# A hybrid trunk on one core: norms' exponential ahead of the decays', spans behind the scaling, and a rearranged last batch of the delta rule

## The chip, the cores and the metric

The kernel runs on one core of one Trainium2 chip. The metric is device microseconds (us) of that core for one launch. Work is done by TensorE (PE; matmuls and, overlapped, weight loads, PEld), VectorE (DVE), ScalarE (ACT), GpSimd (POOL) and by DMA queues, of which SyncE's (SP) carries the weights. Each engine takes its own instructions strictly in order and waits for others through semaphores.

## The reference

A chunk-causal encoder with two layers, sequence 256, width 2048, float32: differential attention, a gated MLP with a causal convolution (ConvFFN), a gated DeltaNet layer, another ConvFFN. The change is in the DeltaNet layer:

```python
proj = h @ w_in                                    # q, k, v, z, and two small gates
qkv = silu(causal_dwconv(qkv, conv_w))
q, k = l2_norm(q), l2_norm(k)                      # 16 heads of 128, each shared by 2 value heads
beta, g = sigmoid(b_gate), -exp(a_log) * softplus(a_gate + dt_bias)
# gated_delta_rule, per value head, in chunks:
g_c = cumsum(g)
decay = exp(where(tril, g_c[:, None] - g_c[None, :], -inf))
low = where(strict, (k * beta) @ k.T * decay, 0)
u, w = triangular_solve(low + eye, v * beta), triangular_solve(low + eye, k * beta * exp(g_c))
...                                                # o: a scan over chunks with a running state
o = rms_norm(o, norm_g) * silu(z)
return o @ w_out
```

## The kernel before

All large products run in three passes (high part of the weight times low and high part of the activation, low part of the weight times high part). Weights stream from HBM in chunks of 512 KB: a load `raw` on SP's queue (L100), a CAST on ACT to `whi` (L111), a subtraction on DVE to `wlo` (L112), then 24 matmuls on PE at L150, L151 and L152 (`ps<-h`, or `ps<-oc` in the DeltaNet's output projection). Four buffers of each rotate. After each chunk `tick` (L81) lets the small tasks that were spawned as generators go on by one step, up to their next `yield`; after a `yield RUN` a task goes on only on every second tick, in the last batch's end on every tick (`self.period`). The steps so put into the program are then ordered per engine by the framework's scheduler. So PE works through weight matmuls with short stretches of small products in between, and the distance from one stretch of a task to its next is a count of weight matmuls.

In `gdn` (L565) the 16 query/key heads are done in four batches (`nb`) of four (`hb`), and in each batch come: four projections for q and k, each followed by a spawned `keys`; a projection for v; two for the gate z; three more for v. After a batch, the output projection `out` of the batch before runs; after the last batch also its own. The tasks:

- `keys(hq, ...)` squares q and k of a head (`cv`, tile `qs`), splits the squares (L323, L324), sums them on PE (L331), takes logarithms (L638, L639) and the exponential (L640) on ACT, and scales `cv` by the result (L645, DVE). PE's products L652 and L653 need the scaled `cv`. Beside this the decays: `gb` is loaded from DRAM on SP's queue (L623, one buffer), DVE makes the spans `d` from it (L633), and ACT takes their exponentials (L643, L644). The products are multiplied by `d` into `lt` and `qkt` (L658, L659).
- `invert` and `join` solve the triangular systems of all heads of a batch, on DVE and then on PE (L718, L727, L741, L750).
- `to_tokens` turns v to tokens (PE L763, ACT L764) and appends to the list `ready`. 
- `group` (two heads, four value heads; two groups in a batch) makes the outputs: products L781, copies L786 and L793, squares L804, sums L805, reciprocal root by Ln and Exp (`rsqrt`, L318, L319), the gate by `zt` (L815), transposes L826, and the split of the result into `oc` (L831 on ACT, L832 on DVE), which the output projection multiplies.

`lnexp` (L297) loads the activation table that holds both Ln and Exp (shown at L299) behind a named instruction and puts what stands in its block behind that load; table loads that other functions need are put in where the order wants them and appear under the line of the function.

Of the kernel before, what the change touches and what calls it, by code (L numbers as in the profile page):

```python
# [8 lines left out]
F32 = mybir.dt.float32  # L9
F32R = mybir.dt.float32r  # L10
AF = mybir.ActivationFunctionType
ALU = mybir.AluOpType
# [4 lines left out]
P = 128  # L17
T = 256
# [11 lines left out]
class Trunk:  # L30
# [38 lines left out]
    def mp(self):  # L69
        return self.mps.tile([P, 512], F32, tag="mp", name="mp")  # L70
# [494 lines left out]
    def gdn(self, w_gate, w_in, w_z, w_out, nb, hb, gate_ap, const_ap, fold_ap, conv_col, ng, done):  # L565
# [7 lines left out]
        nc, tc, mp = self.nc, self.tc, self.mp  # L573
# [4 lines left out]
        with tc.tile_pool(name="gd", bufs=1) as gd:  # L578
# [4 lines left out]
            ident, mask, triu = con[:, :P], con[:, P:T], con[:, T:]  # L583
# [30 lines left out]
            def keys(hq, c, cc, b0, res):  # L614

                sq = gd.tile([P, 2, T], F32, tag="qs", name="qs", bufs=2)
                nc.scalar.square(sq, c)
                sp = gd.tile([P, 2, 2, T], F32R, tag="qp", name="qp", bufs=1)
                self.split(sp, sq)
                while "col" not in gates:  # L620
                    yield
                gb, gc = gd.tile([P, 2 * T], F32, tag="gb", name="gb", bufs=1), gates["col"]
                nc.sync.dma_start(gb.rearrange("p (v t) -> p v t", v=2),  # L623
                                  decays[2 * hq:2 * hq + 2, :].unsqueeze(0).to_broadcast([P, 2, T]))
                yield
                yield
                ds = []
                for v in range(2):
                    h = 2 * hq + v
                    g = gb[:, v * T:(v + 1) * T]  # L630
                    d = gd.tile([P, 384], F32, tag="d", name="d", bufs=2)
                    for t in range(2):
                        nc.vector.scalar_tensor_tensor(  # L633
                            d[:, (1 - t) * P:(2 - t) * P], g[:, t * P:(t + 1) * P], gc[:, t, h:h + 1], mask, ALU.add, ALU.add)
                    ds.append(d)
                pn = mp()
                with self.lnexp(self.total(pn, [sp])):
                    nc.scalar.activation(sq[:, 0, :], pn[:, :T], AF.Ln, bias=eps128, scale=float(P))  # L638
                    nc.scalar.activation(sq[:, 1, :], pn[:, T:], AF.Ln, bias=self.eps, scale=1.0)  # L639
                    nc.scalar.activation(sq, sq, AF.Exp, scale=-0.5)  # L640
                    for v, d in enumerate(ds):
                        h = 2 * hq + v
                        nc.scalar.activation(d[:, :T], d[:, :T], AF.Exp)  # L643
                        nc.scalar.activation(d[:, T:], gb[:, v * T + P:(v + 1) * T], AF.Exp, bias=gc[:, 0, h:h + 1])  # L644
                nc.vector.tensor_tensor(c, c, sq, ALU.mult)  # L645
                q, k = c[:, 0, :], c[:, 1, :]
                yield
                yield RUN
                prods = []
                for r in (k, q):  # L650
                    p = mp()
                    self.nc.tensor.matmul(p[:, :P], k[:, P:], r[:, P:], start=True, stop=True)  # L652
                    self.nc.tensor.matmul(p[:, P:384], k[:, :P], r, start=True, stop=True)  # L653
                    prods.append(p)
                for v in range(2):
                    lt = gd.tile([P, 384], F32, tag="lt", name="lt", bufs=2 * hb)
                    qkt = gd.tile([P, 384], F32, tag="qkt", name="qkt", bufs=2 * hb)
                    nc.vector.tensor_tensor(lt, prods[0][:, :384], ds[v], ALU.mult)  # L658
                    nc.vector.tensor_tensor(qkt, prods[1][:, :384], ds[v], ALU.mult)  # L659
                    b = b0 + v  # L660
                    lv = lt[:, :T].rearrange("p (t c) -> p t c", t=2)
                    for r in quad:
                        nc.gpsimd.tensor_copy(
                            cc[r, :, 2 * b:2 * b + 2].rearrange("p c t -> p t c"), lv[r, :, r])
                    res.append((lt, qkt))

            def invert(cc, lqs, mark):

                while len(lqs) < 2 * hb:
                    yield  # L670
                x = gd.tile([P, 32, 32], F32, tag="s4", name="X", bufs=3)
                nc.vector.transpose(x.rearrange(flat), cc.rearrange(flat))
                t = gd.tile([P, 32, 32], F32, tag="s4", name="Ti", bufs=3)
                nc.vector.tensor_scalar(t, x, -1.0, None, ALU.mult)
                nc.vector.memset(t.rearrange(flat)[:, ::33], 1.0)
                for j in range(1, 31):
                    m = 31 - j
                    tmp = gd.tile([P, T], F32, tag="tmp", name="tmp", bufs=1)
                    w = tmp[:, :m * j].rearrange("p (i c) -> p i c", c=j)
                    nc.vector.tensor_tensor(  # L680
                        w, x[:, j + 1:, j:j + 1].to_broadcast([P, m, j]),
                        t[:, j:j + 1, :j].to_broadcast([P, m, j]), ALU.mult)
                    nc.vector.tensor_tensor(t[:, j + 1:, :j], t[:, j + 1:, :j], w, ALU.subtract)
                    if j % 3 == 0:
                        yield
                ttc = gd.tile([P, 32, 32], F32, tag="s4", name="ttc", bufs=3)
                nc.vector.transpose(ttc.rearrange("p m i -> p i m"), t)
                tcc = gd.tile([P, 32, 32], F32, tag="s4", name="tcc", bufs=3)
                nc.vector.transpose(tcc.rearrange("p m c -> p c m"), t.rearrange("p i c -> p c i"))
                yield from join(lqs, ttc, tcc, mark)  # L690

            using, joined = set(), []

            def join(lqs, ttc, tcc, mark):

                while using:
                    yield
                nm = 2 * gv
                sets = range(len(lqs) // gv)
# [67 lines left out]
            def group(gi, gr, lqs, mark, vt, ready, zts, acts):  # L767

                TT = TTs[gi]
                n = 2 * len(gr)  # L770
# [22 lines left out]
                nc.scalar.copy(w1[:, :n, :], prod([(lambda v: TT[:, 2 * v, :], r1)]))  # L793
                using.discard((mark, gi))
                s = gd.tile([P, 2, gv], F32, tag="os", name="os", bufs=2)
                os = []
                for t in range(2):
# [6 lines left out]
                    nc.scalar.square(sq[:, :n, :], o)  # L804
                    last = nc.vector.tensor_reduce(s[:, t, :n], sq[:, :n, :], AX.X, ALU.add)  # L805
                    os.append(o)
                with self.lnexp(last):
                    self.rsqrt(s[:, :, :n], s[:, :, :n], P)
                while gi not in zts:
                    yield  # L810
                ys = []
                for t in range(2):
                    y = zts[gi][:, t]
                    for v in range(n):
                        nc.vector.scalar_tensor_tensor(  # L815
                            y[:, v, :], os[t][:, v, :], s[:, t, v:v + 1], y[:, v, :], ALU.mult, ALU.mult)
                    ys.append(y)
                yield
                yield RUN
                turned = {}  # L820
# [25 lines left out]
            for b in range(nb):  # L846
                heads = range(b * hb, (b + 1) * hb)
                cc = gd.tile([P, 32, 32], F32, tag="s4", name="Cc", bufs=3)
                nc.gpsimd.memset(cc, 0.0)
                lqs, acts, zts, ready = [], [], {}, []  # L850
                groups = [range(i, i + gh) for i in range(0, hb, gh)]
                plan = [("k", i) for i in range(hb)] + [("v", 0)] + [("z", g) for g in range(len(groups))]
                for op, i in plan + [("v", i) for i in range(1, hb)]:
                    last = b == nb - 1 and op != "k"
                    self.period = 1 if last else 2
                    if op == "k":
                        hq = heads[i]
                        c = convs(lin(self.dense(w_in[hq * 2], KD, self.h_acts, HP)), (hq, nq + hq))
                        self.spawn(keys(hq, c, cc, 2 * i, lqs))
                        if i == hb - 1:  # L860
                            self.spawn(invert(cc, lqs, b))
# [232 lines left out]
```

## Time and profile before

| | us |
|---|---|
| median of 3 runs | 2635.73 (2634.09 to 2637.54) |
| the profiled execution's own time | 2632.3 |
| its span | 2630.5 |
| PE busy | 2619.4 |
| DVE busy | 1835.5 |
| ACT busy | 1444.2 |

In the rows of the timelines, the columns are the start in us, the duration, engine, line and operation, the tile written and the tiles read, shapes, and the count of instructions that the row puts together; a bracket gives the time the engine was idle ahead of it and what released it. In the rows of waits: engine, tile and line that waited, what it waited for, us in total, times, the longest.

### The profile page before, as it was taken

Reading aid. Unit: us, or ns where it says so; the run is one execution under the profiler, and the core shown is the slowest. Engines: PE = TensorE matmul, PEld = TensorE weight load, DVE = VectorE, ACT = ScalarE, POOL = GpSimd, SP = SyncE. Lnnn points to the kernel's source line nnn. Section 1 sums busy time; section 2 is a strip of 40 time slices with the busy share of each in tenths; the row PEclk is TensorE's granted clock in tenths of the full one; section 3 lists DMA queues with packets and bytes.
Section 4 is the critical chain, followed back from the end, with each engine's and each line's share of the span. In section 5 each row is a group of like instructions: output and inputs, shape, how many; then the busy total and the mean of one; then the engine's idle time right before and its main releaser. Section 6 shows DMA issues by size and latency. Waiting matters only on the chain.

```text
span 2630.5 us, 53532 instructions
## 1 busy us (share of the span) xinstructions
PE 2619.4 (100%) x22302; PEld 2561.7 (97%) x22302; DVE 1835.5 (70%) x2718; ACT 1444.2 (55%) x1990; POOL 93.2 (4%) x188
## 2 busy tenths in 40 slices
PE   9999999999999999999999999999999999999999
PEld 9998899999999999999989989989999999999999
DVE  7866667777777555679688787688677777776444
ACT  6665555555555444485764664664555555554333
POOL 0000000000000000011011011021000000000000
PEclk9999999999999999999999999999999999999999
DMA  7565566666666666656455465565466666666665
GB/s 247 168 176 169 163 198 194 194 193 194 193 196 195 190 196 194 188 173 199 137 183 178 137 192 162 164 184 169 143 192 195 195 194 193 193 194 200 199 203 152
DMA packets 138100, 485.34 MB, mean 185 GB/s; under 512 B 15712, under 2 KB 19584, under 8 KB 137856
## 3 DMA queue, kind: packets, MB, share of 16 engines
q1 hardware_dynamic: 137280, 481.42, 60.2%
q8 instruction: 174, 2.85, 0.4%
q14 instruction: 70, 0.57, 0.1%
q10 hardware_dynamic: 576, 0.49, 0.1%
HBM read 479.72 MB, written 2.13 MB: 183 GB/s over the span
## 4 chain that ended last, share of the span: by engine, by line
PE 98%; ACT 1%; DVE 1%; DMA 1%; issue 0%; SPq 0%; DVEq 0%; ACTq 0%
PE ps L150 27%; PE ps L151 27%; PE ps L152 27%; PE ps L237 10%; PE mp L781 1%; PE ps L194 1%; PE mp L331 1%; PE mp L653 0%; PE mp L741 0%; PE mp L750 0%; PE mp L763 0%; PE mp L652 0%; PE mp L471 0%; PE mp L509 0%; DMA raw<-w_first 0%
## 5 line engine op out<-in xcount | busy, mean ns | idle before, releaser
L112 DVE TENSOR_TENSOR wlo<-raw,whi 128x1024 fp32r<-128x1024 f32 (+1 forms) x903 | 1100.6, 1220 | 607.2 <-ACT whi L111 604.3
L111 ACT CAST whi<-raw 128x1024 fp32r<-128x1024 f32 (+1 forms) x903 | 943.9, 1047 | 998.9 <-PE ps L151 829.4
L151 PE MATMUL ps<-h,whi 128*128 128x256 f32 x4224 | 1167.7, 276 | 0.0
L150 PE MATMUL ps<-h,whi 128*128 128x256 f32 x4224 | 1167.7, 276 | 0.0
L152 PE MATMUL ps<-h,wlo 128*128 128x256 f32 x4224 | 1167.4, 276 | 0.0
L152 PEld LDWEIGHTS ps<-h,wlo 128*128 128x128 f32 x4224 | 792.9, 188 | 1.1
L151 PEld LDWEIGHTS ps<-h,whi 128*128 128x128 f32 x4224 | 792.9, 188 | 1.0
L150 PEld LDWEIGHTS ps<-h,whi 128*128 128x128 f32 x4224 | 792.9, 188 | 1.0
L152 PE MATMUL ps<-ac,wlo 128*128 128x256 f32 x1632 | 450.4, 276 | 0.0
L151 PE MATMUL ps<-ac,whi 128*128 128x256 f32 x1632 | 450.4, 276 | 0.0
L150 PE MATMUL ps<-ac,whi 128*128 128x256 f32 x1632 | 450.2, 276 | 0.0
L151 PEld LDWEIGHTS ps<-ac,whi 128*128 128x128 f32 x1632 | 306.4, 188 | 0.0
L152 PEld LDWEIGHTS ps<-ac,wlo 128*128 128x128 f32 x1632 | 306.4, 188 | 0.0
L150 PEld LDWEIGHTS ps<-ac,whi 128*128 128x128 f32 x1632 | 306.2, 188 | 0.0
L237 PE MATMUL ps<-whi,h 128*128 128x512 f32 x768 | 240.1, 390 | 0.0
L237 PEld LDWEIGHTS ps<-whi,h 128*128 128x128 f32 x768 | 143.7, 188 | 30.2
L237 PE MATMUL ps<-wlo,h 128*128 128x512 f32 x384 | 149.8, 390 | 0.0
L150 PE MATMUL ps<-oc,whi 128*128 128x256 f32 x512 | 143.5, 280 | 1.6 <-DVE oc L832 1.6
L151 PE MATMUL ps<-oc,whi 128*128 128x256 f32 x512 | 143.1, 279 | 0.0
L312 DVE SCALAR_TENSOR_TENSOR cv<-u,fcols,cv 128x255 f32<-128x255 f32 (+1 forms) x344 | 142.8, 477 | 0.0
L152 PE MATMUL ps<-oc,wlo 128*128 128x256 f32 x512 | 142.2, 278 | 0.0
L157 DVE TENSOR_TENSOR u<-ps,rstd 128x512 f32<-128x512 f32 x118 | 81.5, 690 | 47.5 <-PE ps L152 47.2
(213 smaller groups left out, 2043.9 us busy)
## 6 DMA issues: line engine op xcount, KB each, us to landing
raw<-w_up SPq DMA_DIRECT2D x344, 512.0 KB, 4.4
raw<-w_down SPq DMA_DIRECT2D x160, 512.0 KB, 3.7
raw<-w_in SPq DMA_DIRECT2D x128, 512.0 KB, 4.2
raw<-w_z SPq DMA_DIRECT2D x64, 512.0 KB, 3.9
raw<-w_out SPq DMA_DIRECT2D x64, 512.0 KB, 3.7
raw<-w_qk SPq DMA_DIRECT2D x56, 512.0 KB, 4.2
raw<-w_v SPq DMA_DIRECT2D x32, 512.0 KB, 3.6
raw<-w_o SPq DMA_DIRECT2D x32, 512.0 KB, 4.3
```

The lines of the kernel that those rows point to most:

```text
L111: self.cast = nc.scalar.copy(hi, raw)
L112: self.low = nc.vector.tensor_tensor(lo, raw, hi.bitcast(F32), ALU.subtract)
L150: nc.tensor.matmul(o, hi[:, k, s], a[:, 1, :], start=first, stop=False)
L151: nc.tensor.matmul(o, hi[:, k, s], a[:, 0, :], start=False, stop=False)
L152: nc.tensor.matmul(o, lo[:, k, s], a[:, 0, :], start=False, stop=last)
L157: self.nc.vector.tensor_tensor(u, ps[:, :, :T], self.rstd.unsqueeze(1).to_broadcast([P, 2, T]), ALU.mult)
L194: self.nc.tensor.matmul(pss[c // 2][:, c % 2, :T], l[:, k, c * P:(c + 1) * P], acts(k0 + k)[:, i, :], start=k0 + k == 0 and l is hi and i ...
L237: self.nc.tensor.matmul(ps[:, c, :], l, r[:, k, :], start=first and not j, stop=last and j == 2)
L312: nc.vector.scalar_tensor_tensor(out[:, j:], u[:, :T - j], taps[n - 1 - j], out[:, j:], ALU.mult, ALU.add)
L331: last = self.nc.tensor.matmul(out, self.onesr, p[:, j], start=i + j == 0, stop=i + j == n)
L781: self.nc.tensor.matmul(p[:, v, :], l(v), r[:, v, :], start=i == 0, stop=i == len(terms) - 1)
```

## The change

There are three edits, all in `gdn`. In `keys` the scaling of `cv` and the norms' exponential are written ahead of the decays' exponentials, and the latter are put behind the former by `issue_after`; for the first two heads (`hq < 2`) the spans come behind the scaling, for the others they stay ahead of the norm sums. In the last batch (`mark == nb - 1`) `join` waits until all four v of the batch are turned to tokens. And in the last batch `group` does the root and the gate for each half of the tokens right after that half's product, and only the first of the four roots has a table load put ahead of it.

```diff
@@ keys
-                ds = []
-                for v in range(2):
-                    ...
-                    ds.append(d)
+                ds = [gd.tile([P, 384], F32, tag="d", name="d", bufs=2) for _ in range(2)]
+
+                def spans():
+                    ...
+                if hq > 1:
+                    spans()
                 pn = mp()
                 with self.lnexp(self.total(pn, [sp])):
                     nc.scalar.activation(sq[:, 0, :], pn[:, :T], AF.Ln, bias=eps128, scale=float(P))
                     nc.scalar.activation(sq[:, 1, :], pn[:, T:], AF.Ln, bias=self.eps, scale=1.0)
-                    nc.scalar.activation(sq, sq, AF.Exp, scale=-0.5)
-                    for v, d in enumerate(ds):
-                        ...
-                nc.vector.tensor_tensor(c, c, sq, ALU.mult)
+                    first = nc.scalar.activation(sq, sq, AF.Exp, scale=-0.5)
+                    unit = nc.vector.tensor_tensor(c, c, sq, ALU.mult)
+                    if hq < 2:
+                        with tc.issue_after(unit.ins):
+                            spans()
+                    with tc.issue_after(first.ins):
+                        for v, d in enumerate(ds):
+                            h = 2 * hq + v
+                            nc.scalar.activation(d[:, :T], d[:, :T], AF.Exp)
+                            nc.scalar.activation(d[:, T:], gb[:, v * T + P:(v + 1) * T], AF.Exp, bias=gc[:, 0, h:h + 1])
@@ join
-                while using:
+                while using or mark == nb - 1 and len(ready) < hb:
                     yield
@@ group
+                end = mark == nb - 1
                 os = []
+
+                def scale(ts, last):
+                    with self.lnexp(last) if not end or (gi, ts.start) == (0, 0) else nullcontext():
+                        self.rsqrt(s[:, ts, :n], s[:, ts, :n], P)
+
+                def gate(t):
+                    ...
                 for t in range(2):
                     ...
                     os.append(o)
-                with self.lnexp(last):
-                    self.rsqrt(s[:, :, :n], s[:, :, :n], P)
+                    if end:
+                        scale(slice(t, t + 1), last)
+                        gate(t)
+                if not end:
+                    scale(slice(0, 2), last)
                 while gi not in zts:
                     yield
-                ys = []
-                ...
+                ys = [zts[gi][:, t] if end else gate(t) for t in range(2)]
```

The new lines shift the old: the exponential of the norms is L643 in the changed kernel (L640 before), the logarithms L641 and L642, the scaling L644 (L645), the spans L634 (L633), the decays' exponentials L651 and L652 (L643, L644), the squares L824 (L804), sums L825 (L805), gates L813 (L815), the split of the result L848 and L849 (L831, L832).

DVE, head 0. Before, the spans `d` stand between the split of the squares and the scaling of `cv`:

```order
L324 TENSOR_TENSOR qp<-qs,qp 128x512
L633 SCALAR_TENSOR_TENSOR d<-gb,gc,con 128x128 x4
L312 SCALAR_TENSOR_TENSOR cv<-u,cols,cv 128x255 x2
L645 TENSOR_TENSOR cv<-cv,qs 128x512
L312 SCALAR_TENSOR_TENSOR cv<-u,cols,cv 128x254
```

The same place of the changed kernel (L312 is the convolution of the next head):

```order
L324 TENSOR_TENSOR qp<-qs,qp 128x512
L312 SCALAR_TENSOR_TENSOR cv<-u,cols,cv 128x255 x2
L312 SCALAR_TENSOR_TENSOR cv<-u,cols,cv 128x254
L644 TENSOR_TENSOR cv<-cv,qs 128x512
L634 SCALAR_TENSOR_TENSOR d<-gb,gc,con 128x128 x4
```

The scaling now stands ahead of the spans, behind one more step of the next head's convolution.

ACT, head 4, the first of the second batch. Before, the decays' exponentials stand between the logarithms and the norms' exponential:

```order
L786 COPY w_15257<-mp 128x512
L299 ACT_TABLE_LOAD
L638 ACTIVATE qs<-mp,eps_13045 128x256
L639 ACTIVATE qs<-mp,eps 128x256
L643 ACTIVATE d<-d 128x256
L644 ACTIVATE d<-gb,gc 128x128
L643 ACTIVATE d<-d 128x256
L644 ACTIVATE d<-gb,gc 128x128
L323 CAST qp<-qs 128x512
L111 CAST whi<-raw 128x1024
L611 ACT_TABLE_LOAD
L611 ACTIVATE cv<-cv 128x512
L640 ACT_TABLE_LOAD
L640 ACTIVATE qs<-qs 128x512
```

And ACT of the changed kernel at that place:

```order
L793 COPY w_15257<-mp 128x512
L299 ACT_TABLE_LOAD
L641 ACTIVATE qs<-mp,eps_13045 128x256
L642 ACTIVATE qs<-mp,eps 128x256
L323 CAST qp<-qs 128x512
L111 CAST whi<-raw 128x1024
L611 ACT_TABLE_LOAD
L611 ACTIVATE cv<-cv 128x512
L643 ACT_TABLE_LOAD
L643 ACTIVATE qs<-qs 128x512
L651 ACTIVATE d<-d 128x256
```

The four exponentials of `d` come behind the norms' exponential. Head 1 has such a sequence too in the changed kernel, with a third table load where it had two.

ACT, the last group of the last batch. Before, both halves are squared, then one root follows, with a table load and CASTs in between:

```order
L793 COPY vt<-mp 128x512
L804 ACTIVATE osq<-mp 128x512 x2
L111 CAST whi<-raw 128x1024
L299 ACT_TABLE_LOAD
L318 ACTIVATE os<-os,eps 128x8
L111 CAST whi<-raw 128x1024
L319 ACTIVATE os<-os 128x8
L111 CAST whi<-raw 128x1024
L831 ACTIVATE oc<-mp,cols 128x2x256 x2
```

In the changed kernel both groups end together, each half with a root of its own:

```order
L824 ACTIVATE osq<-mp 128x512
L319 ACTIVATE os<-os 128x4
L111 CAST whi<-raw 128x1024
L318 ACTIVATE os<-os,eps 128x4
L319 ACTIVATE os<-os 128x4
L824 ACTIVATE osq<-mp 128x512 x2
L318 ACTIVATE os<-os,eps 128x4
L319 ACTIVATE os<-os 128x4
L318 ACTIVATE os<-os,eps 128x4
L319 ACTIVATE os<-os 128x4
L111 CAST whi<-raw 128x1024 x2
L848 ACTIVATE oc<-mp,cols 128x2x256 x3
```

The table load and the CAST between the last sum and its root are gone from there, and the second group's work follows the first's directly.

More of the change, by code (lines that the diff above doesn't have):

```diff
@@ L626, in keys @@
                 yield
-                ds = []
-                for v in range(2):
[L629 to L634, printed above, removed]
-                    ds.append(d)
+                ds = [gd.tile([P, 384], F32, tag="d", name="d", bufs=2) for _ in range(2)]
+                def spans():
+                    for v, d in enumerate(ds):
+                        h = 2 * hq + v
+                        g = gb[:, v * T:(v + 1) * T]
+                        for t in range(2):
+                            nc.vector.scalar_tensor_tensor(
+                                d[:, (1 - t) * P:(2 - t) * P], g[:, t * P:(t + 1) * P], gc[:, t, h:h + 1], mask, ALU.add, ALU.add)
+                if hq > 1:
+                    spans()
                 pn = mp()
@@ L639, in keys @@
                     nc.scalar.activation(sq[:, 1, :], pn[:, T:], AF.Ln, bias=self.eps, scale=1.0)
-                    nc.scalar.activation(sq, sq, AF.Exp, scale=-0.5)
-                    for v, d in enumerate(ds):
[L642 to L645, printed above, removed]
+                    first = nc.scalar.activation(sq, sq, AF.Exp, scale=-0.5)
[4 more added lines that the diff above has]
+                    with tc.issue_after(first.ins):
+                        for v, d in enumerate(ds):
+                            h = 2 * hq + v
+                            nc.scalar.activation(d[:, :T], d[:, :T], AF.Exp)
+                            nc.scalar.activation(d[:, T:], gb[:, v * T + P:(v + 1) * T], AF.Exp, bias=gc[:, 0, h:h + 1])
                 q, k = c[:, 0, :], c[:, 1, :]
@@ L665, in keys, with invert @@
                     res.append((lt, qkt))
-            def invert(cc, lqs, mark):
+            def invert(cc, lqs, mark, ready):
                 while len(lqs) < 2 * hb:
@@ L689, in invert, with join @@
                 nc.vector.transpose(tcc.rearrange("p m c -> p c m"), t.rearrange("p i c -> p c i"))
-                yield from join(lqs, ttc, tcc, mark)
+                yield from join(lqs, ttc, tcc, mark, ready)
             using, joined = set(), []
-            def join(lqs, ttc, tcc, mark):
-                while using:
+            def join(lqs, ttc, tcc, mark, ready):
+                while using or mark == nb - 1 and len(ready) < hb:
                     yield
@@ L795, in group @@
                 s = gd.tile([P, 2, gv], F32, tag="os", name="os", bufs=2)
+                end = mark == nb - 1
                 os = []
+                def scale(ts, last):
+                    with self.lnexp(last) if not end or (gi, ts.start) == (0, 0) else nullcontext():
+                        self.rsqrt(s[:, ts, :n], s[:, ts, :n], P)
+                def gate(t):
+                    y = zts[gi][:, t]
+                    for v in range(n):
+                        nc.vector.scalar_tensor_tensor(
+                            y[:, v, :], os[t][:, v, :], s[:, t, v:v + 1], y[:, v, :], ALU.mult, ALU.mult)
+                    return y
                 for t in range(2):
@@ L806, in group @@
                     os.append(o)
-                with self.lnexp(last):
-                    self.rsqrt(s[:, :, :n], s[:, :, :n], P)
+                    if end:
[3 more added lines that the diff above has]
+                    scale(slice(0, 2), last)
                 while gi not in zts:
                     yield
-                ys = []
[L812 to L817, printed above, removed]
+                ys = [zts[gi][:, t] if end else gate(t) for t in range(2)]
                 yield
@@ L860, in gdn @@
                         if i == hb - 1:
-                            self.spawn(invert(cc, lqs, b))
+                            self.spawn(invert(cc, lqs, b, ready))
                     elif op == "z":
```

## The prediction

> **What bounds the kernel now.** I read the page's head first, then PE's list of waits, then the timelines around each of them.
>
> ```profile
> span 2630.5 us, 53532 instructions
> PE 2619.4 (100%) x22302; PEld 2561.7 (97%) x22302; DVE 1835.5 (70%) x2718; ACT 1444.2 (55%) x1990; POOL 93.2 (4%) x188
> ```
>
> TensorE is busy for 2619.4 of 2630.5 us, and the change gives it the same 21509 instructions as before. So the edit can win only places where PE stands still in the delta-rule layer. Three rows of its waits are all there is:
>
> ```profile
> PE mp L652 <- DVE cv L645: 2.0, 3, 1.0
> PE mp L826 <- DVE zt L815: 1.8, 1, 1.8
> PE ps L150 <- DVE oc L832: 1.6, 1, 1.6
> ```
>
> Five waits, 5.4 us. In PE's timeline (start, duration, instruction, idle time and releaser in brackets) they are:
>
> ```profile
> 1142.27 0.28 PE L150 MATMUL ps<-h,whi 128*128 128x256 f32 x1
> 1143.17 0.49 PE L652 MATMUL mp<-cv 128*128 128x128 f32 x2 [0.63 <-DVE cv L645]
> ...
> 1152.77 0.28 PE L150 MATMUL ps<-h,whi 128*128 128x256 f32 x1
> 1153.79 0.28 PE L150 MATMUL ps<-h,whi 128*128 128x256 f32 x1
> 1154.50 0.49 PE L652 MATMUL mp<-cv 128*128 128x128 f32 x2 [0.43 <-DVE cv L645]
> ...
> 1303.94 0.46 PE L652 MATMUL mp<-cv 128*128 128x128 f32 x2 [0.95 <-DVE cv L645]
> ...
> 1881.49 0.28 PE L152 MATMUL ps<-oc,wlo 128*128 128x256 f32 x1
> 1883.57 1.09 PE L826 MATMUL mp<-con,zt 128*128 128x128 f32 x8 [1.80 <-DVE zt L815]
> 1886.22 0.39 PE L150 MATMUL ps<-oc,whi 128*128 128x256 f32 x1 [1.56 <-DVE oc L832]
> ```
>
> The rows at 1152.77 and 1153.79 are the first and the last of ten matmuls in a run: 1.02 / 9 = 0.113 us from start to start when nothing is waited for. I price a wait by starts: 1143.17 - 1142.27 - 0.113 = 0.79 us for head 0, where the bracket says 0.63, so a wait costs some 0.16 more than its bracket (the pipeline drains, 0.28 against 0.113). Head 1: 1154.50 - 1153.79 - 0.113 = 0.60. Head 4: 0.95 + 0.165 = 1.12. The last group's transposes: 1883.57 - 1881.49 - 0.113 = 1.97. The first product of the last projection's next block: 1.56 + 0.16 = 1.72. Sum 6.2 us: the ceiling of the gain as far as waits go.
>
> **Head 0 (spans behind the scaling).** DVE and then ACT ahead of the first wait:
>
> ```profile
> 1136.83 0.69 DVE L324 TENSOR_TENSOR qp<-qs,qp 128x512 fp32r<-128x512 f32 x1 [0.72 <-ACT qp L323]
> 1140.59 1.14 DVE L633 SCALAR_TENSOR_TENSOR d<-gb,gc,con 128x128 f32<-128x128 f32 x4 [3.07 <-DMA gb<-decays]
> 1141.65 0.87 DVE L312 SCALAR_TENSOR_TENSOR cv<-u,cols,cv 128x255 f32<-128x255 f32 x2
> 1142.44 0.68 DVE L645 TENSOR_TENSOR cv<-cv,qs 128x512 f32<-128x512 f32 x1
> ...
> 1137.50 0.62 ACT L640 ACTIVATE qs<-qs 128x512 f32<-128x512 f32 x1
> ```
>
> The norms' factor (L640) is ready at 1138.12, yet the scaling L645 runs at 1142.44: DVE takes its work in order, and the spans L633 stood for 3.07 us for the transfer of gb. In the new order of DVE two L312 come after L324, then the scaling, then the spans. The L312 take some 0.9-1.3 us from 1137.5, so the scaling can run at about 1138.9-1139.6. PE comes to its L652 six weight matmuls earlier than before, at 1142.27 + 0.113 - 0.7 = 1141.7. Slack 2 us: the wait is gone, 0.79 us won. What queues behind the spans now is L312 of the next head and the weight splits; the spans still wait for gb until 1140.6, as before, and L652 no longer depends on them. The products that need the decays (L658, L659 of before) come after L653 as they did. Cost 0; ends 0 and 0.79.
>
> **Heads 1 and 4 (norms' exponential ahead of the decays').** ACT, head 4 of before:
>
> ```profile
> 1294.40 1.28 ACT L299 ACT_TABLE_LOAD   x1
> ...
> 1296.42 0.41 ACT L643 ACTIVATE d<-d 128x256 f32<-128x256 f32 x1
> ...
> 1297.62 0.61 ACT L323 CAST qp<-qs 128x512 fp32r<-128x512 f32 x1
> 1298.13 1.05 ACT L111 CAST whi<-raw 128x1024 fp32r<-128x1024 f32 x1
> 1299.20 1.28 ACT L611 ACT_TABLE_LOAD   x1
> 1300.50 0.63 ACT L611 ACTIVATE cv<-cv 128x512 f32<-128x512 f32 x1
> 1301.14 1.28 ACT L640 ACT_TABLE_LOAD   x1
> 1302.44 0.63 ACT L640 ACTIVATE qs<-qs 128x512 f32<-128x512 f32 x1
> ```
>
> Between the two logarithms and the exponential L640 stand four decays' exponentials, from 1296.42 to 1297.62 = 1.20 us. The new order has the same nine other rows and the four after L640. So the chain from the table load to PE, 1303.94 - 1294.40 = 9.54 us, becomes 8.34. PE's own distance is nearly unchanged: in the new order 52 weight matmuls (5.9 us) and 12 products of about 0.22 us lie between the norm sums and L652, 8.6-8.7 us; the load starts some 0.6 us after the sums, behind the copy of w. So PE waits 8.34 + 0.6 - 8.65 = 0.3, where it waited 1.12. I take 0.2 (ends 0 and 0.5), since PE's six-matmul shifts elsewhere do not reach here: 0.9 won.
>
> Head 1 changes more: its chain gets a third table load (load, two logarithms, CAST, load, silu, load, exponential). From the rows just shown, without the 1.20 and without L323's 0.51: 8.67 - 1.71 = 6.96 us from the first load to the exponential's end, 0.7 for the scaling and 0.15 to PE, 7.8. The order gives PE 71 weight matmuls between sums and L652, 71 x 0.113 = 8.05. Slack 0.2, so 0.60 won; ends 0 (a load that comes 0.8 late) and 0.60. The other thirteen heads lose 1.20 us or less of their chains and, by the same count, keep 1.7 us or more.
>
> On the loads there is a rule that speaks against this step. The row first: the load at 1299.20 starts 0.02 us after the CAST's end, and the silu starts 1300.50 - 1299.20 = 1.30 later, so a switch costs 1.30 us here. The Trainium skill, "ScalarE: Activation LUTs", in its account of the table load, puts about 1380 ns of draining on top of 1283 ns, 2.66 us in all for each switch. By its figure three switches would make head 1 some 4 us late; by the row nothing. The measurement decides, and the trace does not agree with the rule.
>
> **The last batch (join held back, each half scaled by itself).** Rows of PE's last product, ACT and DVE in the end of the last group before:
>
> ```profile
> 1875.27 0.39 PE L781 MATMUL mp<-vt,qkt 128*128 128x128 f32 x2
> ...
> 1875.69 0.60 ACT L804 ACTIVATE osq<-mp 128x512 f32<-128x512 f32 x1 [3.56 <-PE mp L781]
> 1878.65 0.30 ACT L318 ACTIVATE os<-os,eps 128x8 f32<-128x8 f32 x1
> 1880.09 0.20 ACT L319 ACTIVATE os<-os 128x8 f32<-128x8 f32 x1
> ...
> 1876.66 0.68 DVE L805 TENSOR_REDUCE os<-osq 128x4 f32<-128x512 f32 x1
> 1881.36 2.15 DVE L815 SCALAR_TENSOR_TENSOR zt<-mp,os,zt 128x128 f32<-128x128 f32 x8
> ...
> 1885.42 1.41 DVE L832 SCALAR_TENSOR_TENSOR oc<-mp,cols,oc 128x512 fp32r<-128x512 f32 x2 [0.78 <-ACT oc L831]
> ```
>
> From the last product (end about 1875.6) to the last gate (1883.5) go 7.9 us, through a square, a sum, a table load, logarithm, two CASTs and eight gates. PE had 51 weight matmuls, 5.8 us. In the new order, counted from the last product: square to 0.7, sum to 1.4, logarithm and root to 2.0 with no load and no CAST between, and four gates (half of 2.15, 1.08) to 3.1; the first group's four may stand ahead, 3.6 at most. PE has 48 weight matmuls = 5.4 us to the first of 16 transposes, and the last group's eight come 0.9 later. Slack 1.8-2.8 us: 1.97 won. After the transposes PE has 24 weight matmuls more (2.7 us) of the block before, which it can run on what stood ready; from the transposes' end oc takes a copy 0.7, a weight split in between 1.2 and 0.7 for L832, some 1.5 us inside that reach; the second group's half is needed 48 matmuls later still. 1.72 won.
>
> The price is that all four chains of the batch's join now start after the last v, at one place. In the new order the stages L763, L718, L727, L741, L750 and L781 (lines of before) follow each other with 38, 26, 28, 21 and 45 weight matmuls between, 2.4 us at the least; PE's list above has no row at any of these lines, in none of the four batches. I cost this at 0; its bounds are 0 and one wait of the size seen, 1.97. PE's way back to the weights costs something too:
>
> ```profile
> 1875.41 0.37 PE L150 MATMUL ps<-oc,whi 128*128 128x256 f32 x1
> 1875.61 0.28 PE L151 MATMUL ps<-oc,whi 128*128 128x256 f32 x1
> ```
>
> The first gap is 0.20 instead of 0.113. The batch breaks PE's run of weights 12 times where it was 15, so 3 x 0.09 = 0.3 us less, which I leave out of the sum.
>
> **Sum.** 0.79 + 0.60 + 0.9 + 1.97 + 1.72 = 6.0 us. The profiled execution's own time is 2632.3 (span 2630.5), so 2626.3 there. The median of the runs is 2635.73, 3.4 above it, so 2629.7 by the median. 0.2% is 5.3 us, about what a measurement of this kernel tells from no change; the forecast lies only just beyond it, and the chances are split for that reason.
>
> **Rivals.**
>
> Part of the waits stays. Heads 1 and 4 have slacks of 0.2 and -0.2 us, which is less than the length of any instruction in their chains: one CAST (1.05) put ahead by other arrival times brings 0.4-0.9 back at each. In the last batch the same holds for oc, slack 1.5 against a weight split of 1.2. With one or two of these the gain is 3-5 us: 2630.8-2632.7. For it: slacks smaller than a CAST. Against it: only one of the three is large.
>
> A wait in place of the removed one. If the held-back join makes PE stand at L741 or L763 as it did at L826, 2 us for each of two groups, the last batch wins nothing: gain 2, 2633.7. Against it: no such row before.
>
> The extra load is dearer than 1.30. If each of head 1's three loads took another load's time behind it, it is 3.8 us late and the gain is 6.0 - 0.6 - 3.6 = 1.8: 2633.9. Against it: the two loads of head 4's rows stand without a gap.
>
> Slower: the decays' exponentials come later on ACT, and they free gb, whose next load sits in SP's queue ahead of the weights.
>
> ```profile
> SPq L623 <- DVE d L633: 23.9, 11, 4.3
> SPq L623 <- ACT d L644: 12.3, 5, 4.4
> ...
> ACT whi L111 <- DMA raw<-w_in: 1.8, 2, 1.1
> ...
> raw<-w_in SPq DMA_DIRECT2D x128, 512.0 KB, 4.2
> ```
>
> SP stood behind gb's release up to 4.4 us at a time already, and ACT waited for those weights only twice, at most 1.1, with PE not waiting at all. Another 1 us (from 0.65 to 2 for L640's time and its wait) on each of the 12 heads from the second batch on would have to pass straight to PE to give 12 - 6 = 6 us slower, 2641.7. It decides from the point at which SP's hold passes the lead of the four weight buffers: four chunks of 24 matmuls are 10.9 us, less the 4.2 of a landing, some 6.7 us, against 4.4 + 1.
>
> **How the numbers follow.** Forecast 0.52; part stays 0.30; a new wait in the last batch 0.08; dear loads 0.04; slower 0.06. The predicted time is the forecast's, 2629.7. Its own range is 2627.5-2631, from the ceiling of 6.2 + 0.3, the kept 0.5 at head 4, and the scatter of the three runs (2634.09 to 2637.54, 1.7 to a side). For eight in ten I take 2627 to 2634, which leaves out the slower case and the outermost of the others. Faster by over 0.2% means under 2630.46: most of the forecast, little of the second case, 0.53. Within 0.2%: 0.41. Slower 0.06.
>
> **What would show it.** Each row of PE's waits answers for a step: the one for L652 on the scaling should fall from three times 2.0 us to at most one below 0.5; those for L826 and for the product on oc should be gone; no new row over 0.5 should stand in the layer. DVE's wait for gb stays, behind the scaling. ACT should show 52 loads of 1.28. SP's waits for d may grow by some us with no row at PE. The forecast is wrong if PE's waits fall by 5 us and the time does not, or if a row for L741, L750 or L763 appears.

## The result and the profile after

| | before | changed |
|---|---|---|
| median of 10 runs, us | 2634.82 (2633.65 to 2638.83) | 2628.78 (2627.18 to 2629.29) |
| span of the profiled execution, us | 2630.5 | 2627.2 |

The ratio is 0.9973, 95% interval 0.9965 to 0.9982: 6.0 us faster by the medians, 4.7 to 9.2 by the interval.

The head of the changed kernel's page, and then all of its waits on PE:

```profile
span 2627.2 us, 53543 instructions
PE 2619.0 (100%) x22302; PEld 2561.7 (98%) x22302; DVE 1838.3 (70%) x2718; ACT 1447.1 (55%) x1995; POOL 89.5 (3%) x188
```

```profile
PE ps L194 <- ACT whi L111: 2.6, 1, 2.6
PE mp L76 <- DVE eps L52: 1.0, 1, 1.0
PE ps L237 <- DVE wlo L112: 0.6, 1, 0.6
PE ps L194 <- DVE whi L166: 0.5, 1, 0.5
PE ps L194 <- ACT whi L170: 0.4, 1, 0.4
```

The three rows of before that the change aimed at, 5.4 us together, are gone. The rows at L76 and L194 lie in the first 11 us, where the programs are the same. One row in the layer is new: a product for z (L237) waits 0.56 us for a weight split.

Since PE runs its matmuls back to back, the traces can be laid side by side by the count of weight matmuls. The time of each stretch, less that of the profiled execution of before (the ends of a stretch are places where the small products done so far are the same; worked out from PE's starts in the traces):

| weight matmuls | what is there | changed, us |
|---|---|---|
| 0 to 200 | first loads | +1.65 |
| 200 to 9150 | attention, its ConvFFN, the layer's start | +0.01 |
| 9150 to 9500 | heads 0 and 1 | -1.08 |
| 9500 to 10500 | second batch, head 4 first | +0.04 |
| 10500 to 13300 | third batch, rest of the fourth's heads | +0.01 |
| 13300 to 14000 | last batch's end | -3.83 |
| 14000 to end | ConvFFN | 0.00 |

So the change is worth 4.85 us in this pair of traces, at two of the three places, and 6.0 by the medians. The profiled execution of before took 2632.3 us, and of the 91 timed runs of before, here and in the three series below, 85 took longer. The 1.65 at the start is an accident of the execution: over thirteen profiled executions of this study, all with the same program there, that stretch lay between -0.5 and +1.65 against before's.

Head 0, on DVE and ACT of the changed kernel:

```profile
1138.37 0.69 DVE L324 TENSOR_TENSOR qp<-qs,qp 128x512 fp32r<-128x512 f32 x1 [0.72 <-ACT qp L323]
1138.98 1.27 DVE L312 SCALAR_TENSOR_TENSOR cv<-u,cols,cv 128x255 f32<-128x255 f32 x3
1140.17 0.68 DVE L644 TENSOR_TENSOR cv<-cv,qs 128x512 f32<-128x512 f32 x1
1142.29 1.14 DVE L634 SCALAR_TENSOR_TENSOR d<-gb,gc,con 128x128 f32<-128x128 f32 x4 [1.44 <-DMA gb<-decays]
...
1139.04 0.62 ACT L643 ACTIVATE qs<-qs 128x512 f32<-128x512 f32 x1
```

The scaling starts 1140.17, 0.51 after the exponential's end and 2.12 ahead of the spans, which still wait for gb. Head 1 has its third table load, on ACT and then the scaling on DVE and the products on PE:

```profile
1148.31 1.28 ACT L611 ACT_TABLE_LOAD   x1
1149.60 0.63 ACT L611 ACTIVATE cv<-cv 128x512 f32<-128x512 f32 x1
1150.25 1.28 ACT L643 ACT_TABLE_LOAD   x1
1151.55 0.63 ACT L643 ACTIVATE qs<-qs 128x512 f32<-128x512 f32 x1
...
1152.21 0.69 DVE L644 TENSOR_TENSOR cv<-cv,qs 128x512 f32<-128x512 f32 x1 [1.73 <-ACT qs L643]
...
1153.54 0.38 PE L659 MATMUL mp<-cv 128*128 128x128 f32 x2
```

The scaling ends 1152.90 and PE comes at 1153.54 with no wait. Head 4 still has the table load ahead of its exponential, but the decays' exponentials no longer:

```profile
1304.01 1.28 ACT L643 ACT_TABLE_LOAD   x1
1305.30 0.63 ACT L643 ACTIVATE qs<-qs 128x512 f32<-128x512 f32 x1
...
1305.96 0.69 DVE L644 TENSOR_TENSOR cv<-cv,qs 128x512 f32<-128x512 f32 x1 [2.31 <-ACT qs L643]
...
1306.77 0.44 PE L659 MATMUL mp<-cv 128*128 128x128 f32 x2
```

The scaling ends 1306.65, 0.12 us ahead of the products. The last batch's end: PE's last product, ACT's roots, DVE's gates, the transposes and oc:

```profile
1867.46 0.39 PE L788 MATMUL mp<-vt,qkt 128*128 128x128 f32 x2
...
1869.56 0.21 ACT L319 ACTIVATE os<-os 128x4 f32<-128x4 f32 x1
...
1869.12 2.15 DVE L813 SCALAR_TENSOR_TENSOR zt<-mp,os,zt 128x128 f32<-128x128 f32 x8
...
1873.14 1.91 PE L843 MATMUL mp<-con,zt 128*128 128x128 f32 x16
...
1875.45 1.40 DVE L849 SCALAR_TENSOR_TENSOR oc<-mp,cols,oc 128x512 fp32r<-128x512 f32 x2
```

The gates end 1871.27, 3.4 us after the last product (it was 7.9), and the transposes start 1.9 us behind them. oc is split by 1876.85, under 1 us ahead of its first use.

### The profile page after: what moved, and what is told of

Same layout as the page of the kernel before. It is cut to its first block, busy times and chain, and to the rows that moved or that the text cites. A ratio compares the mean times of both kernels' runs of the same rounds, so it can differ in the third digit from the quotient of the medians.

```text
span 2627.2 us, 53543 instructions
## 1 busy us (share of the span) xinstructions
PE 2619.0 (100%) x22302; PEld 2561.7 (98%) x22302; DVE 1838.3 (70%) x2718; ACT 1447.1 (55%) x1995; POOL 89.5 (3%) x188
## 4 chain that ended last, share of the span: by engine, by line
PE 98%; ACT 1%; DVE 0%; DMA 0%; issue 0%; SPq 0%; DVEq 0%; ACTq 0%
PE ps L150 27%; PE ps L152 27%; PE ps L151 27%; PE ps L237 10%; PE mp L788 1%; PE ps L194 1%; PE mp L331 1%; PE mp L660 0%; PE mp L757 0%; PE mp L748 0%; PE mp L770 0%; PE mp L843 0%; PE mp L471 0%; PE mp L509 0%; DMA raw<-w_first 0%; PE mp L659 0%
## 5 line engine op out<-in xcount | busy, mean ns | idle before, releaser
L237 PE MATMUL ps<-whi,h 128*128 128x512 f32 x768 | 239.8, 390 | 0.0
L237 PEld LDWEIGHTS ps<-whi,h 128*128 128x128 f32 x768 | 143.7, 188 | 30.2
L237 PE MATMUL ps<-wlo,h 128*128 128x512 f32 x384 | 149.8, 390 | 0.6 <-DVE wlo L112 0.6
L312 DVE SCALAR_TENSOR_TENSOR cv<-u,fcols,cv 128x255 f32<-128x255 f32 (+1 forms) x344 | 142.8, 477 | 0.0
```

Source lines behind the costliest of these rows:

```text
L237: self.nc.tensor.matmul(ps[:, c, :], l, r[:, k, :], start=first and not j, stop=last and j == 2)
L312: nc.vector.scalar_tensor_tensor(out[:, j:], u[:, :T - j], taps[n - 1 - j], out[:, j:], ALU.mult, ALU.add)
```

## The experiments

All are built from before or from the changed kernel; the tables and rows are of one profiled execution each, the times of 6 to 11 runs. Medians of before in the three series: 2635.19, 2634.59, 2635.89 us.

**Which edit brings what.** Four kernels take the change apart: the edit of `keys` alone, the last batch's edits alone, the held join alone, the roots by halves alone.

```diff
 # e1: keys as changed, invert, join and group as before
 # e2: keys as before, invert, join and group as changed
 # e3, on before (`ready` is also handed down through invert)
-                while using:
+                while using or mark == nb - 1 and len(ready) < hb:
 # e4, on before (the main lines; the rest of the edit of group with them)
+                    if end:
+                        scale(slice(t, t + 1), last)
+                        gate(t)
```

> Only the edit of the keys task (norms' exponential ahead of the decays', spans behind the scaling for the first two heads); the last batch as before. Theory A: the three waits at the products of q and k vanish (2.5 us by starts), and the one new wait that the changed kernel shows (a product of z waiting 0.56 us for a weight split at 1326 us, with 0.4 us of more frequent returns) comes with them, because ACT has two more table loads and the late decays' exponentials in a row just ahead: 1.1 us faster net, waits at the last group's transposes (1.8) and on oc (1.6) unchanged. Rival B, as the prediction's sum had it: 2.3 us faster, the z wait an accident of one execution and absent here.

> Only the last batch's two edits (join held back, root and gate for each half); keys as before. Theory A (edits add up): 3.7 to 3.8 us faster, the rows for the transposes and for oc gone, three waits at the products of q and k of 2.0 us as before, no z wait. Rival B: the last batch's gain needs the keys edit; then one of the two rows stays and the gain is under 2 us.

> Only the join of the last batch held back; one root for both halves as before. Theory A (both edits needed): the chain from the last product to the gates stays long, so a wait of 1 us or more is left at the transposes or on oc; 1 to 2 us faster. Rival B (the hold does it all): PE's order now has 63 weight matmuls, 7.1 us, between the last product and the first transposes, and the first group's gates are done by about 6.5; only the wait on oc may stay, 0 to 0.7; 3.0 to 3.7 us faster.

> Only root and gate for each half in the last batch; join not held. Theory A: the chain after the last product shrinks from 7.9 to about 3.6 us, the transposes' wait (1.97 by starts) is gone, but oc is needed right behind the transposes as before: its wait of 1.6 stays; 2.0 us faster. Rival B: the half-by-half roots alone bring the whole 3.7 us, with both rows gone.

| | median us | ratio, interval | heads 0, 1 | second batch | last batch |
|---|---|---|---|---|---|
| e1 | 2632.25 | 0.9994, 0.9985 to 1.0002 | -1.08 | -0.01 | -0.28 |
| e2 | 2629.25 | 0.9975, 0.9966 to 0.9984 | +0.91 | +0.02 | -3.83 |
| e3 | 2630.03 | 0.9982, 0.9974 to 0.9991 | +0.45 | +0.02 | -3.38 |
| e4 | 2631.15 | 0.9987, 0.9978 to 0.9995 | +0.28 | 0.00 | -1.90 |

The last three columns are stretches of the trace as in the table above, against before's. PE's waits in the layer, of e1, e2, e3 and e4 in turn:

```profile
PE ps L150 <- DVE oc L839: 1.6, 1, 1.6
PE mp L833 <- DVE zt L822: 1.5, 1, 1.5
...
PE ps L237 <- DVE wlo L112: 0.6, 1, 0.6
```

```profile
PE mp L652 <- DVE cv L645: 3.0, 3, 1.6
```

```profile
PE mp L652 <- DVE cv L645: 2.1, 2, 1.1
...
PE ps L150 <- DVE oc L832: 0.2, 1, 0.2
```

```profile
PE ps L150 <- DVE oc L842: 2.1, 1, 2.1
...
PE mp L652 <- DVE cv L645: 1.9, 2, 1.0
```

e1 has the z wait and the other three do not: it comes with the edit of `keys`, so Theory A, and it was no accident. In e2 the last batch wins 3.83 by itself. e3 goes against my Theory A and bears out Rival B: the hold does nearly all alone (-3.38 of -3.83). It moves PE's last products ahead, so that the long chain with its table loads has 63 weight matmuls to hide behind, and all that remains is 0.2 us on oc. The roots by halves alone clear the transposes, but not oc, whose wait even grows to 2.1. The two edits overlap: 3.38 + 1.90 is 5.3, more than there was to win. The -0.28 of e1 in the last batch, where its program is that of before, is a wait at the transposes of 1.5 us instead of 1.8. The times by runs have intervals that are wide beside effects of 1 us, and they show more than the traces: e2's -3.8 lies outside its interval, which begins at -4.2. This is so for all twelve changed kernels: their columns add up to 1.2 to 3.7 us less than their medians show, and the profiled execution that they are compared with was 2.3 to 3.6 us faster than the medians of before.

The heads 0 and 1 column differs between e2, e3 and e4, whose program there is that of before. DVE's spans in e2:

```profile
1141.40 1.14 DVE L633 SCALAR_TENSOR_TENSOR d<-gb,gc,con 128x128 f32<-128x128 f32 x4 [4.02 <-DMA gb<-decays]
```

The gb transfer lands at another moment of PE's run in each execution: the wait for it was 3.07, 4.02, 3.56 and 3.35 us in before, e2, e3 and e4, and PE's stretch longer by 0.91, 0.45 and 0.28 than in before's own execution, which had the shortest wait of the four. With the mean, 0.41, the edit wins about 1.5 us there, not 1.08.

**The parts of the keys edit.** e5 holds each head's silu behind the norms' exponential of the head before; e6 keeps the spans ahead for all heads, e7 puts them behind for all; e8 puts a table load ahead of all four roots of the last batch.

```diff
 # e5, on the changed kernel (behind: the norms' exponential of the head before)
+                with tc.issue_after(behind.ins) if behind else nullcontext():
+                    nc.scalar.activation(c, c, AF.Silu)
 # e6, on the changed kernel (and no spans behind the scaling)
-                if hq > 1:
-                    spans()
+                spans()
 # e7, on the changed kernel (and no spans ahead of it)
-                    if hq < 2:
+                    if True:
 # e8, on the changed kernel
-                    with self.lnexp(last) if not end or (gi, ts.start) == (0, 0) else nullcontext():
+                    with self.lnexp(last):
```

> The changed kernel, with the silu of a head's q and k held behind the norms' exponential of the head before it in the same batch, so that no silu (with its two table loads) stands between a head's logarithms and its exponential; 50 table loads instead of 52. Theory A: the new wait on z (0.56 us, 0.7 by starts) came from the two additional loads in ACT's row ahead of the weights' CAST; here it is gone, head 4's chain gets some 1.9 us shorter, no new wait at the products of q and k: 0.7 to 1 us faster than the changed kernel, 6 to 7 us faster than before. Rival B: it came from the decays' exponentials, late and all together ahead of the CAST; the z wait stays, same time as the changed kernel. Rival C: the silu held back makes the next head late: a wait of 1 us or more at its products.

> The changed kernel, with the spans ahead of the norm sums for the first two heads too, as before; the norms' exponential still ahead of the decays'. Theory A: head 0's wait comes back in full, since DVE stands at the spans for gb whatever ACT does (0.8 to 1.7 us by starts, as in the four executions with the old keys), head 1's does not, since there gb is long landed. 0.8 to 1.7 us slower than the changed kernel. Rival B: the order on ACT alone frees both heads; no row for the products of q and k.

> The changed kernel, with the spans behind the scaling for all sixteen heads; so gb is freed later on all of them, 60 table loads instead of 52. Theory A: gb and the decays have slack and SP's hold stays inside the lead of the weight buffers; waits of SP for the spans and the decays' exponentials grow, PE's do not: within 0.5 us of the changed kernel, apart from single waits under 1 us behind the additional loads. Rival B (the prediction's slower case): the later release of gb holds the weights up, with rows of 1 us or more for the weights on PE: 3 us or more slower.

> The changed kernel, with a table load ahead of each of the four roots of the last batch instead of the first alone (55 loads). Theory A: the chain after the last product has 1.8 us or more of slack; two loads of 1.28 on it and a CAST eat that up and leave a wait of 0 to 1.5 us at the transposes or on oc: 0 to 1.5 us slower than the changed kernel. Rival B: if a load cost 2.66 us in all, two loads on the chain would be 5.3 us, and the waits 2.5 us or more.

| | median us | ratio, interval | heads 0, 1 | second batch | third and on | last batch |
|---|---|---|---|---|---|---|
| e5 | 2634.59 | 0.9999, 0.9991 to 1.0008 | +0.28 | -3.00 | +7.96 | -3.83 |
| e6 | 2629.01 | 0.9980, 0.9971 to 0.9989 | +0.48 | -0.31 | +0.03 | -3.83 |
| e7 | 2630.20 | 0.9985, 0.9976 to 0.9994 | -1.07 | -0.96 | +3.19 | -3.71 |
| e8 | 2628.22 | 0.9974, 0.9964 to 0.9984 | -1.08 | +0.04 | +0.01 | -3.63 |

e6: head 0's wait is back (1.27 us by starts, bracket 1.11) and head 1's is not:

```profile
1143.45 0.49 PE L655 MATMUL mp<-cv 128*128 128x128 f32 x2 [1.11 <-DVE cv L643]
```

So at head 0 it is DVE's order that counts; at head 1, where the spans are early as well, it is not. Its second batch has another order too, with no wait on z and one of 0.7 at head 4, although the decays' exponentials stand behind the norms' there as in the changed kernel: the chain's first load starts 1.27 us after the end of the norm sums, in the changed kernel 0.44 us.

e7: the second batch wins the whole 0.96. In the third and the fourth, PE waits at the norm sums and, once, at a head's products:

```profile
PE mp L331 <- ACT qp L323: 0.9, 3, 0.5
PE mp L657 <- DVE cv L642: 0.7, 1, 0.7
...
SPq L623 <- DVE d L634: 33.4, 15, 4.2
...
ACT whi L111 <- DMA raw<-w_in: 1.7, 2, 1.1
```

The first two rows are of PE, the third of SP's queue, the last of ACT. SP's hold for the spans grew from the changed kernel's 14.3 to 33.4 us, and ACT's wait for the weights is 1.7, in the changed kernel 1.8: the prediction's slower case does not happen even with gb freed late on every head. What is late is ACT itself, with eight more table loads, for the split of the next head's squares. Theory A had single waits under 1 us right, but not what they add up to: by the columns e7 is 2.3 us slower than the changed kernel.

e5 and e11 (below) have a wait of 3.2 us on the silu of z. On ACT and PE of e11:

```profile
1368.23 0.58 ACT L771 COPY vt<-mp 128x512 f32<-128x512 f32 x1 [0.70 <-PE mp L770]
1368.82 1.28 ACT L884 ACT_TABLE_LOAD   x1
1370.12 2.42 ACT L884 ACTIVATE zt<-ps,rstd 128x512 f32<-128x512 f32 x4
...
1371.44 0.38 PE L150 MATMUL ps<-h,whi 128*128 128x256 f32 x1 [3.24 <-ACT zt L884]
```

The silu that empties z's banks stands behind the copy of v, and PE's next product needs those banks. In the changed kernel it stands behind that copy too; but there the transposes of v that the copy waits for come at weight matmul 10505, here and in e5 at 10544, just ahead of that product. So the large wait of e5 came at another place than rival C named; besides it, e5 has a wait of 0.7 us at a head's products next to it, of 1.0 at norm sums in the first batch, and of 1.2 at the gates ahead of head 0, which is in no column here.

The twelve small products at that place are in the second column for the changed kernel and in the third for e5 and e11, and are worth some 1.8 us (if the stretches are cut at matmul 10500 itself, ahead of which the changed kernel lacks them and before has them, its two columns read -1.76 and +1.81). So the two columns of e5 and e11 mean something only together, +4.96 and +4.51; with the 1.8 put back, the second batch by itself wins some 1.2 us in either, somewhat more than Theory A of e5 said.

e8: the loads on the chain cost 0.2 us of the last batch, no row on PE. ACT there:

```profile
1867.30 1.28 ACT L299 ACT_TABLE_LOAD   x1
1868.60 0.30 ACT L318 ACTIVATE os<-os,eps 128x4 f32<-128x4 f32 x1
1868.91 1.28 ACT L299 ACT_TABLE_LOAD   x1
1870.21 0.30 ACT L318 ACTIVATE os<-os,eps 128x4 f32<-128x4 f32 x1
```

The logarithm starts 1.30 us after the load's start, both times, and the next load 0.01 us after the logarithm's end. These loads bring the same set again; the switches between sets in head 1's rows above, silu to exponential, take the same 1.30. That does not agree with the 2.66 us for a switch in the Trainium skill, "ScalarE: Activation LUTs", under "What ACT_TABLE_LOAD costs".

**What the z wait is made of, and a faster kernel.** In before, ACT has head 5's exponential ahead of the next silu's table load:

```profile
1311.24 0.62 ACT L640 ACTIVATE qs<-qs 128x512 f32<-128x512 f32 x1
...
1317.41 1.28 ACT L611 ACT_TABLE_LOAD   x1
```

ACT of the changed kernel between head 5's logarithms and the product that waits, with the weight split on DVE and PE behind it:

```profile
1314.22 1.28 ACT L611 ACT_TABLE_LOAD   x1 [1.29 <-DVE cv L312]
...
1317.46 0.63 ACT L643 ACTIVATE qs<-qs 128x512 f32<-128x512 f32 x1
...
1323.79 1.04 ACT L111 CAST whi<-raw 128x1024 fp32r<-128x1024 f32 x1
...
1325.13 1.22 DVE L112 TENSOR_TENSOR wlo<-raw,whi 128x1024 fp32r<-128x1024 f32 x1
...
1326.40 0.49 PE L237 MATMUL ps<-wlo,h 128*128 128x512 f32 x1 [0.56 <-DVE wlo L112]
```

ACT stands 1.29 us for the silu's input, since its order has the silu ahead of head 5's exponential; then come a second load, the exponential and the decays' exponentials, and ACT is busy without a gap up to the CAST at 1323.79 that the waiting product needs. Three kernels keep the silu out of that place in other ways.

```diff
 # e9, on the changed kernel; e10 has 5 for 8
-                if hq > 1:
+                if hq >= 8:
-                    if hq < 2:
+                    if hq < 8:
 # e11, on the changed kernel
-                    with tc.issue_after(first.ins):
+                    with tc.issue_after(first.ins) if hq < 2 else nullcontext():
```

> The changed kernel, with the spans behind the scaling for the heads of the first two batches (eight heads instead of two), the later ones as in the changed kernel. Engines' orders are those of e7 through the second batch, where no silu stands between head 5's logarithms and its exponential, and PE's order is that of the changed kernel behind it. Theory A (the z wait came from the silu and its load ahead of head 5's exponential, which hold the weights' CAST back): no z wait, no wait at head 4's products, heads 0 and 1 and the last batch as in the changed kernel: 1.0 us faster than it. Rival B: the later release of gb brings waits of its own in the second batch, as e7 had them in the third: not faster than the changed kernel.

> As e9, with the spans behind the scaling for the first five heads alone; 51 table loads instead of 52. Theory A: as e9, since head 4 is the last with little slack; 1.0 us faster than the changed kernel, no wait on z. Rival B: with head 5's spans early, the decays' exponentials of that head come ahead of the weights' CAST and the z wait is back, 0.7 us.

> The changed kernel, with the order of norms' and decays' exponentials bound only for the first two heads; for the others the scheduler sets it. It puts head 4's four decays' exponentials ahead again, but the norms' exponential ahead of the next head's silu, so that no table load stands in that chain. Theory A: what holds head 4 is two table loads and a silu (3.2 us) more than the decays' exponentials (1.2): no wait at head 4's products, no silu ahead of head 5's exponential and no z wait; 0.5 to 1.1 us faster than the changed kernel. Rival B: the decays' exponentials are what mattered: head 4's wait of about 1 us is back, same time as the changed kernel or slower.

| | median us | ratio, interval | heads 0, 1 | second batch | third and on | last batch |
|---|---|---|---|---|---|---|
| e9 | 2626.83 | 0.9970, 0.9959 to 0.9982 | -1.07 | -0.95 | +0.01 | -3.83 |
| e10 | 2626.39 | 0.9967, 0.9955 to 0.9979 | -1.07 | -0.95 | +0.01 | -3.83 |
| e11 | 2632.03 | 0.9987, 0.9979 to 0.9996 | -1.11 | -2.95 | +7.46 | -3.83 |

e9 and e10 have no wait of PE in the layer at all. The same place on ACT of e10:

```profile
1311.91 0.63 ACT L643 ACTIVATE qs<-qs 128x512 f32<-128x512 f32 x1
...
1316.16 1.28 ACT L611 ACT_TABLE_LOAD   x1
...
1320.65 1.03 ACT L111 CAST whi<-raw 128x1024 fp32r<-128x1024 f32 x1
```

The exponential comes ahead of the silu's load. The CAST at 1320.65 is that of the chunk that PE waited for; it starts 3.8 us ahead of its product, in the changed kernel 2.6, the wait included. e10 has head 5's decays' exponentials as early as the changed kernel and no z wait, so its Rival B is out. Over all thirteen traces, the silu stands ahead of head 5's exponential in the three kernels with the z wait (the changed one, e1, e8) and behind it in the ten without. In their traces e9 and e10 are both 1.0 us faster than the changed kernel, at the place named; by the medians 2.0 and 2.4, but the intervals of the ratios overlap with the changed kernel's. They are the fastest kernels here. e11 freed head 4 too, with the four decays' exponentials back ahead of the norms': there is no wait at its products and no z wait, so either is enough to take out: the decays' exponentials, as in the changed kernel, or the two loads and the silu, as here. The wait on z's banks then took more than was won.

## Why the prediction was right, and which of its steps were off

All five waits went, and by the mechanism told. At four of them the time went with them; at head 4 it came back as a new wait, and that term came to nothing. That the sum of 6.0 is also the difference of the medians is luck: in the traces, where the terms were read, the change wins 4.85, and the medians add what made before's other executions slower than its profiled one.

- **Head 0:** as worked out. The spans still wait for gb, and PE does not wait for them. The scaling started 1140.17 for a PE that was 1.5 us later than in before's trace; e6 shows the DVE order to be the cause.
- **Head 1:** no wait. Its slack was 0.64 us, not 0.2. But heads 0 and 1 together gave 1.08 and not the 1.39 of the waits: PE breaks off its run of weights 9 times in this stretch where it was 6, and three returns of 0.09 are most of the difference. I had counted such returns in the last batch alone.
- **Head 4:** this term failed. I put 0.9 won there, as a smaller wait at L652. The wait did go, altogether, though with 0.12 us to spare; in e6, where the same chain started later, 0.7 us of it is left. But a silu of the following head, with its two table loads, now stands ahead of head 5's exponential and held a weight CAST back, and the z wait came 20 us behind head 4's products. Of 1.15 us won at head 4 the z wait took 0.83, counted up to the start of the next matmul; three gaps of some 0.1 at PE's returns from small products are the rest, and the stretch ends at +0.04. I counted slack for the norm chains of all heads and did not count the CASTs queued behind those chains on ACT. My "part stays" rival had an added CAST in the chain; it was the chain in front of a CAST. My own sign of being wrong, a new row over 0.5 in the layer, did come (0.56).
- **Last batch:** 3.83 against 3.69. The 0.3 for fewer returns, left out of the sum, has the sign of the difference. My slack at the transposes was right (1.9 us); at oc I wrote 1.5, and it is under 1. My own terms there, 0.7 + 1.2 + 0.7 against 2.7 us, leave only 0.1. That both edits are needed, which I implied by pricing them together, is wrong: the held join does 3.38 by itself.
- **The rest of the 6.0:** the sum was made against one execution in which gb came early. Against that trace heads 0 and 1 won 1.08; over the four executions of the old program about 1.5, which makes 5.3 in all, inside the interval of 4.7 to 9.2. What remains to 6.0 is not resolved by these runs.
- **Slower case:** no sign of it; SP's waits for d fell, from 43.6 us in before to 25.6, and e7 pushed the same mechanism further with no late weights. Of the two waits for weights that I quoted against it (1.8 us), both lie ahead of the first gb load; behind it, before has one of 2.1 us, on w_z at 1195.3, which I overlooked, and PE does not wait there either.
- **Dear loads:** no; 1.29 to 1.30 us from a load's start to the next instruction, in five pairs of rows above.
- **The count of PE's instructions:** 21509 is not what the pages say; they have 22302 for both kernels, so that the argument, the same work for PE, stands.

## What to carry to other kernels

Where one engine is busy 100%, list its waits and price them by starts: here the 6.2 us of the list were the ceiling, and the best reordering (e9, e10) won 5.8 in the traces. When a chain on a side engine is reordered, follow what is queued behind it on that engine, the stream of weights first: here 0.8 of the 1.1 us won at one product went again to a late CAST 20 us on. And try to take the wait out by more distance (an earlier or held-back start, as with the join) before shortening the chain: in the last batch distance did 3.4 us where shortening did 1.9.

## What the runs showed that I had not expected

The moment at which gb lands moved PE's wait at head 0 between 0.79 and 1.74 us over executions of one program, and the first 200 weight matmuls varied by 2 us, while the 8950 matmuls behind them agreed to 0.03 us in all traces but two (e8 +0.39, e5 +1.43). So in these traces the scatter outside of the edits sat almost wholly in two places, and stretches of PE's run counted in matmuls resolved effects of 0.1 us that ten timed runs could not.

The timed runs scatter more than that: those of before lie between 2631.3 and 2640.0 us, and one profiled execution does not show where. The six runs of e10, which has no wait of PE left in the layer, lie within 0.9 us, and those of e9 within 1.7. That the waits are what makes before scatter would fit this, but it was not tested.
